# The first norm of an encoder trunk moves from the token rows to the results of the projections, and the first loads change order

## The chip, the core and the metric

The kernel runs on one core of a Trainium2 chip. The metric is device microseconds (us) of one execution; the time of a kernel is the median of its runs. Engines are named as the profile names them: PE multiplies matrices (PEld loads its stationary operand), ACT is the scalar engine, DVE the vector engine, POOL the third elementwise engine, and SP issues every DMA of this kernel. An engine works through its own instructions in order and waits on semaphores of others.

## What is computed

A two-layer encoder on 256 tokens of 1024 features. Only the start of layer 0 (the "even" layer) is touched:

```python
def rms_norm(x, g, eps=EPS):
    y = xf * lax.rsqrt(jnp.mean(xf * xf, axis=-1, keepdims=True) + eps)
    return (y * g.astype(jnp.float32)).astype(x.dtype)

def even_mixer(h, w_in, ...):
    proj = h @ w_in                                   # 1024 -> 1536 + 256 + 128 + 32
    hy, cq, ckv, kr = jnp.split(proj, [c0, c1, c2], axis=-1)
    hy = short_conv(hy, conv_w, conv_b)               # three taps along the tokens
    ...                                               # gated long convolution
    q = (rms_norm(cq, q_norm) @ w_uq)...              # latent attention, queries
    kv = (rms_norm(ckv, kv_norm) @ w_ukv)...          # keys and values
    k_pe = apply_rope(kr[:, :, None, :], cos_r, sin_r)
    ...

x = x + even_mixer(rms_norm(x, norm_mix[0]), ...)
x = x + cross_attention(rms_norm(x, norm_cross[i]), mem_n, ...)
x = x + sq_relu_mlp(rms_norm(x, norm_mlp[i]), ...)
```

After it come cross-attention to 256 memory tokens, an MLP of 4096, the same three blocks for layer 1 (differential attention in place of the even mixer), and a final norm. The norm is a factor per token, `rsqrt(mean(x²) + eps)`, times a gain per feature; a projection is linear, so the factor per token can be put on the projection's result.

## The kernel before

Every large product is made of three: each fp32 operand is split into a high part (rounded to a shorter mantissa, written by ACT, `split`, L104 to L106) and the rest (DVE, L106), and `mm3` (L108 to L112) issues high·high, high·low and low·high into one PSUM bank. A weight tile of up to 128×1024 is loaded by SP into one of four buffers `wraw` (`weight`, L87) and split into one of six pairs `whi`, `wlo`. SP therefore stands before a weight's load until the split of the fourth weight before it is done.

The 256 tokens lie as two tiles `xt[0]`, `xt[1]` of 128 rows (even and odd tokens) in buffers `t4`, of which there are three. For a projection the tokens have to stand transposed, features on the partitions: `h` is a pair (high, low) of 128 × 8 × 256, where index k is a block of 128 features and the last axis holds both token tiles.

PSUM has four banks `h` (function `hb`), three `b` (`wk`) and one `f`.

The stages of layer 0 are written in a string, `ORDER_EVEN` (L30), and issued in that order. A planner of the framework then places the instructions on the engines: it keeps that order as a priority, but an engine that by its own estimate of durations would stand idle gets a later instruction whose inputs are there. So the order on PE, ACT, DVE and SP is fixed when the kernel is built, and on the chip an engine waits for the instruction that is next, even if one behind it could run.

The stages at the start, in the order of the string:

- ahead of them: SP loads one row of gains (4 KB), both x tiles (512 KB each), `cpack` (identity and the gains by column, 92 KB), `c_rope`, the two latent gains `gq`. PE spreads the gain row over the partitions with a product with `ones` (L147) into two banks.
- `N` (`norm_in`): per token tile a Square with row sum on ACT (L183), two small POOL steps (`rstd_of`, L167 and L169), then DVE scales each half row by factor and gain in one step (L188); PE transposes four blocks of 128×128 (L175) and `split` evicts them, for features 0 to 511 of both token tiles.
- `G` (`filter_features`): loads `pack` (250 KB), two small products (L333, L337) each followed by a sine made of eight DVE steps and one ACT step.
- `J` (`lat_proj`): the latent projection, 416 columns, in four weight tiles of 416 KB (`w_lat`), each used for 12 matmuls; the features 512 to 1023 are transposed after the second weight (`mid`).
- `L` (`latents`): the two latent norms, the rotary of the shared key, transposes into `latT`.
- `H0` (`hy_chunk`): the first of six chunks of the Hyena projection, 256 columns each: two weight tiles, 48 matmuls into one bank, then per 128 channels one ACT step (L503) and four DVE steps (L506) of the short convolution, read from the bank.
- `U`, `K`, `R`: queries, keys and values, transposed queries. Later come scores and outputs of the eight heads (`S`, `O`), the filters (`F`, whose weight is `hy_w3`), the spectra (`P`), the other chunks (`H1` to `H5`), and `M`, which normalizes and transposes the memory with the same `normed` (L183, L188).

Of the kernel before, what the change touches and what calls it, by code (L numbers as in the profile page):

```python
# [17 lines left out]
P = 128  # L18
D = 1024
# [6 lines left out]
C2 = float(np.float32(TWO_PI - C1))  # L26
C3 = float(np.float32(TWO_PI - C1 - C2))
PI_LO = 3.1415925
# Order in which the stages are issued: a letter names the stage (see the run() calls), digits are its arguments.
ORDER_EVEN = "N G J L H0 U K R S0 D H1 F0 S1 T0 S2 S3 P0 O0 O1 O2 H2 S4 O3 H3 T1 F1 S5 S6 O4 O5 Y S7 H4 P1 H5 O6 O7 M W"  # L30
ORDER_CROSS = [
    "V0 K0 Q0 K1 S0 V1 B0 K2 S1 Q1 K3 W0 S2 B1 S3 V2 B2 V3 B3 W1",
    "K0 K1 Q0 V0 S0 S1 K2 B0 Q1 K3 S2 V1 B1 V2 B2 W0 V3 S3 B3 W1",
# [5 lines left out]
def tile_encoder(ctx: ExitStack, tc: tile.TileContext, a: dict, out: bass.AP):  # L39
# [17 lines left out]
    def hb():  # L57
        return T(ps, [P, 512], F32, "h", bufs=4)
# [10 lines left out]
    def t4(dt=F32):  # L69
        return T(ring, [P, 1024], dt, "t4", bufs=3)  # L70
# [10 lines left out]
    def col(n=1):  # L81
        return T(cst, [P, n], F32, f"col{n}", bufs=16)
# [1 line left out]
    def v3(t, k):  # L84
        return t.rearrange("p (k n) -> p k n", k=k)

    def weight(src, cols=1024, side=False, gi=None, nk=2):  # L87
        p_, x, nr, nw = (rp, "f", 2, 2) if side else (wp, "w", 4, 6)
        raw = T(p_, [P, 1024], F32, x + "raw", bufs=nr)[:, :cols]
        hi = T(p_, [P, 1024], F32R, x + "hi", bufs=nw)[:, :cols]  # L90
        lo = T(p_, [P, 1024], F32R, x + "lo", bufs=nw)[:, :cols]
        nc.sync.dma_start(raw, src)
        if gi is None:
            split(hi, lo, raw)
            return hi, lo
        gi, k0 = gi
        for k in range(nk):
            g = gcol[:, gi, k0 + k:k0 + k + 1]
            h_, l_, r_ = (v3(z, nk)[:, k, :] for z in (hi, lo, raw))
            nc.scalar.activation(h_, r_, AF.Identity, bias=zero, scale=g)  # L100
            nc.vector.scalar_tensor_tensor(l_, r_, g, h_.bitcast(F32), op0=ALU.mult, op1=ALU.subtract)  # L101
        return hi, lo
# [16 lines left out]
    es = ExitStack()  # L119
    ep = pool("ep", es)  # L120
    cur.update(pool=ep, n2=4)
# [2 lines left out]
    def load_x(dst):  # L124
        for t in range(2):
            nc.sync.dma_start(dst[t], xv[t])

    def const(p_, name, shape, src=None):
        t = T(p_, shape, F32, name)
        nc.sync.dma_start(t, a[name] if src is None else src)  # L130
        return t

    ones = T(ep, [1, P], F32, "ones")
    nc.gpsimd.memset(ones, 1.0)
    grow = t4()[0:1]
    nc.sync.dma_start(grow, a["gains"][0:1])
    xt = [t4(), t4()]
    load_x(xt)

    def gain(src):  # L140
        g = t4()
        nc.sync.dma_start(g, src.partition_broadcast(P))
        return g

    g_mix0 = [hb(), hb()]
    for c in range(2):
        nc.tensor.matmul(g_mix0[c], ones, grow[:, c * 512:(c + 1) * 512], start=True, stop=True)  # L147
    pack = const(cst, "cpack", [P, 184])
    ident = pack[:, :128]
    gcol = pack[:, 128:].rearrange("p (g k) -> p g k", k=8)  # L150
    packe = T(ep, [P, 500], F32, "pack")
# [9 lines left out]
    nc.gpsimd.memset(zero, 0.0)  # L161
    junk = T(cst, [P, D], BF16, "junk")

# [1 line left out]
    def rstd_of(ssq, n, dim, eps):  # L165
        r = col(n)
        nc.gpsimd.tensor_scalar(r, ssq, 1.0 / dim, eps, op0=ALU.mult, op1=ALU.add)  # L167
        r2 = col(n)
        nc.gpsimd.tensor_tensor(r2, r, mhalf[:, :n], op=ALU.pow)  # L169
        return r2  # L170
# [8 lines left out]
    def normed(xs, g):  # L179
        rs = []  # L180
        for x in xs:
            ssq = col()
            nc.scalar.activation(junk, x, AF.Square, accum_out=ssq)  # L183
            rs.append(rstd_of(ssq, 1, D, EPS))
        for t, x in enumerate(xs):
            for c in range(2):
                xc = x[:, c * 512:(c + 1) * 512]
                nc.vector.scalar_tensor_tensor(xc, xc, rs[t], g[c], op0=ALU.mult, op1=ALU.mult)  # L188

    def half_T(xs, h, c, bank=wk):  # L190
        for t, x in enumerate(xs):
            tr_split(x[:, c * 512:(c + 1) * 512], h, t, c, bank)
# [109 lines left out]
    def sin_of(b, bias, dst):  # L302
        y = h2(256)[:b.shape[0]]
        nc.vector.tensor_scalar(y, b, bias, fb[:b.shape[0], 2:3], op0=ALU.add, op1=ALU.mult)
# [96 lines left out]
    def softmax_e(sc, scale=None):  # L401
        s3 = v3(sc, 2)
        nm = col(2)
# [25 lines left out]
        else:  # L429
            split(dst, lo, b3)  # L430

    # ======== even mixer ========
    h = v3(t8(F32R), 8), v3(t8(F32R), 8)

    def tok_major(y):
# [13 lines left out]
    nc.sync.dma_start(gq[:, 256:], a["mla_kv_norm"].partition_broadcast(P))  # L449
    lat = []  # L450

    def norm_in():
        normed(xt, g_mix0)
        half_T(xt, h, 0)

    def lat_proj():
        lat.extend([wk(), wk()])
        proj_xs(h, a["w_lat"], 416, lat, mid=lambda: half_T(xt, h, 1), at=1)

    latT = [T(ep, [P, 3, 256], F32R, f"latT{i}") for i in range(2)]  # L460
    kT = v3(t8(), 8)
# [1 line left out]
    def latents():  # L463
        for t in range(2):
            ln = t2()
            ssq = col(2)
            nc.scalar.activation(ln[:, :256], lat[t][:, :256], AF.Square, accum_out=ssq[:, 0:1])
            nc.scalar.activation(ln[:, 256:384], lat[t][:, 256:384], AF.Square, accum_out=ssq[:, 1:2])
            rq = rstd_of(ssq[:, 0:1], 1, 256, EPS)
            rk = rstd_of(ssq[:, 1:2], 1, 128, EPS)  # L470
            nc.vector.scalar_tensor_tensor(ln[:, :256], lat[t][:, :256], rq, gq[:, :256], op0=ALU.mult, op1=ALU.mult)
            nc.vector.scalar_tensor_tensor(ln[:, 256:384], lat[t][:, 256:384], rk, gq[:, 256:], op0=ALU.mult, op1=ALU.mult)
            kp = T(ep, [P, 96], F32, "kp", bufs=2)
            nc.gpsimd.memset(kp[:, :64], 0.0)
            kr = lat[t][:, 384:416]
            tmp = T(ep, [P, 32], F32, "kptmp", bufs=2)
            nc.vector.tensor_tensor(tmp[:, :16], kr[:, 16:], SM[:, t, :16], op=ALU.mult)
            nc.vector.tensor_tensor(tmp[:, 16:], kr[:, :16], SM[:, t, 16:], op=ALU.mult)
            nc.vector.tensor_tensor(kp[:, 64:], kr, CM[:, t, :], op=ALU.mult)
            nc.vector.tensor_tensor(kp[:, 64:], kp[:, 64:], tmp, op=ALU.add)  # L480
            b = wk()
            for k in range(3):
                nc.tensor.transpose(b[:, k * P:(k + 1) * P], ln[:, k * P:(k + 1) * P], ident)
            nc.tensor.transpose(b[:96, 384:], kp, ident)
            sl = (slice(None), slice(0, 3), slice(t * P, (t + 1) * P))
            split(latT[0][sl], latT[1][sl], v3(b[:, :384], 3))
            nc.scalar.copy(kT[64:96, :, t * P:(t + 1) * P],
                           b[64:96, 384:].unsqueeze(1).to_broadcast([32, 8, P]))
# [3 lines left out]
    def hy_chunk(u):  # L492
        bank = hb if u < 4 else wk
        if u % 2 == 0:
            hyS[u // 2] = T(ep, [P, 4, 256], F32, "hy", bufs=2)
        b = bank()
        proj_w(h, a["w_hy"][u], b)
        for c in range(2):
            ct = 2 * u + c
            src = b[:, c * 256:(c + 1) * 256]  # L500
            y = hyS[ct // 4][:, ct % 4, :]
            w = [conv[:, j, ct:ct + 1] for j in range(4)]
            nc.scalar.activation(y, src, AF.Identity, bias=w[3], scale=w[1])  # L503
            e, o, ye, yo = src[:, :P], src[:, P:], y[:, :P], y[:, P:]
            for dst, s, wt in ((ye, o, w[2]), (yo, e, w[0]), (ye[:, 1:], o[:, :P - 1], w[0]), (yo[:, :P - 1], e[:, 1:], w[2])):
                nc.vector.scalar_tensor_tensor(dst, s, wt, dst, op0=ALU.mult, op1=ALU.add)  # L506
# [103 lines left out]
    def mla_proj():  # L610
        hs["b"] = [[wk(), wk()], [wk(), fl()]]
        proj_down(catm, (0, 1, 2, 3), a["w_out_ev"], (4, 5, 6, 7), hs["b"], True)

    run(ORDER_EVEN, S=mla_s, O=mla_o, H=hy_chunk, F=filters, T=toks, P=spec, Y=conv0, W=mla_proj, M=mem_T,
        N=norm_in, J=lat_proj, L=latents, G=filter_features, U=queries, K=keys_values, R=queries_T, D=tables)
    ys, banks = hs["y"], hs["b"]
    cat = [v3(t8(F32R), 8) for _ in range(2)]
    for u in range(2):
# [385 lines left out]
```

## Time and profile before

| | |
|---|---|
| median of 3 runs | 863.78 us (861.42, 863.78, 863.94) |
| profiled execution | span 861.4 us, beside the run of 861.42 us |
| PE busy | 841.5 us, 5326 matmuls |
| DVE busy | 567.4 us |
| ACT busy | 482.8 us |
| POOL busy | 21.4 us |
| DMA | 139.53 MB, mean 162 GB/s |

The span runs from the first to the last instruction. "Busy" sums the time in which an engine worked; PE's matmuls overlap in the records, so the distance from one start to the next says more of them than the duration of one. In a line of the timeline stand the start, the duration, the engine, the line of the kernel, the operation with output and inputs, how many instructions were merged, and in brackets how long the engine had been idle and what released it. In a line of groups, "x16 | 4.4, 275" means 16 instructions, 4.4 us in all, 275 ns each. A line of windows gives for each engine the busy us and the number of instructions in a stretch of time, then the granted PE clock (1.00 is full), the share of time in which the DMA engines worked, and the GB/s that they moved.

### The profile page before, as it was taken

Reading aid. Unit: us, or ns where it says so; the run is one execution under the profiler, and the core shown is the slowest. Engines: PE = TensorE matmul, PEld = TensorE weight load, DVE = VectorE, ACT = ScalarE, POOL = GpSimd, SP = SyncE. Lnnn points to the kernel's source line nnn. Section 1 sums busy time; section 2 is a strip of 40 time slices with the busy share of each in tenths; the row PEclk is TensorE's granted clock in tenths of the full one; section 3 lists DMA queues with packets and bytes.
Section 4 is the critical chain, followed back from the end, with each engine's and each line's share of the span. In section 5 each row is a group of like instructions: output and inputs, shape, how many; then the busy total and the mean of one; then the engine's idle time right before and its main releaser. Section 6 shows DMA issues by size and latency. Waiting matters only on the chain.

```text
span 861.4 us, 13548 instructions
## 1 busy us (share of the span) xinstructions
PE 841.5 (98%) x5326; PEld 742.0 (86%) x5326; DVE 567.4 (66%) x880; ACT 482.8 (56%) x784; POOL 21.4 (2%) x54
## 2 busy tenths in 40 slices
PE   6999999999999999999999999999999999999996
PEld 4967587999989999999988787789998999999995
DVE  5878986855557655655568889576564765565553
ACT  5864444755447555555467676675443755555542
POOL 0100000000000000000000010200000000000000
PEclk9999999999999999999999999999999999999998
DMA  7550317744344555555536524325432465555531
GB/s 259 201 216 18 118 43 276 259 157 154 117 147 173 195 189 183 191 191 182 191 126 222 171 99 155 139 99 196 149 121 74 167 201 181 187 195 183 185 121 49
DMA packets 39526, 139.53 MB, mean 162 GB/s; under 512 B 4515, under 2 KB 5283, under 8 KB 39462
## 3 DMA queue, kind: packets, MB, share of 16 engines
q1 hardware_dynamic: 39462, 138.66, 46.8%
q8 instruction: 42, 0.69, 0.3%
q14 instruction: 22, 0.18, 0.1%
HBM read 137.59 MB, written 1.05 MB: 161 GB/s over the span
## 4 chain that ended last, share of the span: by engine, by line
PE 86%; issue 7%; DMA 2%; ACT 2%; DVE 1%; POOL 1%; SPq 0%; POOLq 0%; ACTq 0%
PE h L110 14%; PE h L111 14%; PE h L112 14%; PE b L110 11%; PE b L111 10%; PE b L112 10%; PE f L110 2%; PE f L111 2%; PE f L112 2%; PE b L175 1%; DMA t<-in_hy_w_dram 1%; DMA pack<-in_pack_dram 1%; PE b L839 1%; PE b L426 1%; DMA wraw<-in_xa_wk_dram 1%
## 5 line engine op out<-in xcount | busy, mean ns | idle before, releaser
L106 DVE TENSOR_TENSOR wlo<-wraw,whi 128x1024 fp32r<-128x1024 f32 (+2 forms) x131 | 158.5, 1213 | 120.7 <-ACT whi L105 119.9
L105 ACT CAST whi<-wraw 128x1024 fp32r<-128x1024 f32 (+2 forms) x131 | 135.7, 1041 | 146.9 <-PE b L111 58.0
L100 ACT ACTIVATE whi<-wraw,zero,cpack 128x512 fp32r<-128x512 f32 x208 | 159.3, 809 | 66.9 <-PE b L111 33.3
L101 DVE SCALAR_TENSOR_TENSOR wlo<-wraw,cpack,whi 128x512 fp32r<-128x512 f32 x208 | 150.6, 750 | 54.5 <-ACT whi L100 54.2
L110 PE MATMUL b<-t,whi 128*128 128x256 f32 x544 | 154.3, 284 | 0.0
L112 PE MATMUL b<-t,wlo 128*128 128x256 f32 x544 | 154.1, 283 | 0.0
L111 PE MATMUL b<-t,whi 128*128 128x256 f32 x544 | 154.1, 283 | 0.0
L110 PEld LDWEIGHTS b<-t,whi 128*128 128x128 f32 x544 | 104.5, 192 | 0.9 <-issue 0.4
L111 PEld LDWEIGHTS b<-t,whi 128*128 128x128 f32 x544 | 104.5, 192 | 0.5
L112 PEld LDWEIGHTS b<-t,wlo 128*128 128x128 f32 x544 | 104.5, 192 | 0.0
L112 PE MATMUL h<-whi,ul 128*128 128x512 f32 x256 | 100.0, 390 | 0.0
L111 PE MATMUL h<-wlo,uh 128*128 128x512 f32 x256 | 99.9, 390 | 0.0
L110 PE MATMUL h<-whi,uh 128*128 128x512 f32 x256 | 99.9, 390 | 0.0
L110 PE MATMUL h<-whi,t 128*128 128x512 f32 x192 | 77.1, 402 | 0.0
L111 PE MATMUL h<-wlo,t 128*128 128x512 f32 x192 | 76.6, 399 | 0.0
L112 PE MATMUL h<-whi,t 128*128 128x512 f32 x192 | 76.0, 398 | 0.0
L112 PEld LDWEIGHTS h<-whi,ul 128*128 128x128 f32 x256 | 48.1, 188 | 9.9
L110 PE MATMUL h<-t,whi 128*128 128x256 f32 x192 | 55.8, 291 | 0.6 <-ACT t L105 0.6
L110 PEld LDWEIGHTS h<-whi,uh 128*128 128x128 f32 x256 | 48.2, 188 | 9.5
L111 PEld LDWEIGHTS h<-wlo,uh 128*128 128x128 f32 x256 | 48.1, 188 | 9.5
L111 PE MATMUL h<-t,whi 128*128 128x256 f32 x192 | 55.3, 288 | 1.0 <-DVE t L106 1.0
L112 PE MATMUL h<-t,wlo 128*128 128x256 f32 x192 | 55.4, 289 | 0.0
(287 smaller groups left out, 1549.2 us busy)
## 6 DMA issues: line engine op xcount, KB each, us to landing
wraw<-in_mlp_up_dram SPq DMA_DIRECT2D x64, 512.0 KB, 3.3
wraw<-in_mlp_down_dram SPq DMA_DIRECT2D x64, 512.0 KB, 3.2
wraw<-in_od_w_qkv_dram SPq DMA_DIRECT2D x24, 512.0 KB, 4.3
wraw<-in_xa_wq_dram SPq DMA_DIRECT2D x16, 512.0 KB, 4.3
wraw<-in_xa_wo_dram SPq DMA_DIRECT2D x16, 512.0 KB, 3.6
wraw<-in_w_hy_dram SPq DMA_DIRECT2D x12, 512.0 KB, 4.6
wraw<-in_w_out_ev_dram SPq DMA_DIRECT2D x8, 512.0 KB, 4.8
wraw<-in_xa_wv_dram SPq DMA_DIRECT2D x8, 512.0 KB, 4.9
```

Of the source, the lines that this page charges most:

```text
L100: nc.scalar.activation(h_, r_, AF.Identity, bias=zero, scale=g)
L101: nc.vector.scalar_tensor_tensor(l_, r_, g, h_.bitcast(F32), op0=ALU.mult, op1=ALU.subtract)
L105: nc.scalar.copy(hi, src)
L106: nc.vector.tensor_tensor(lo, src, hi.bitcast(F32), op=ALU.subtract)
L110: nc.tensor.matmul(o, lh, rh, start=first, stop=False)
L111: nc.tensor.matmul(o, lh, rl, start=False, stop=False)
L112: nc.tensor.matmul(o, ll, rh, start=False, stop=last)
L175: nc.tensor.transpose(b[:, k * P:(k + 1) * P], x[:, k * P:(k + 1) * P], ident)
L426: nc.tensor.transpose(b3[:, m, t * P:(t + 1) * P], p3[:, t, m * P:(m + 1) * P], ident)
L839: nc.tensor.matmul(ob[:, t * P:(t + 1) * P], aT[:, m, t * P:(t + 1) * P], vo[j][:, m, c * P:(c + 1) * P], start=m == 0, stop=m == 1)
```

## The change

The stage `N` goes; `J` now stands first in the order, ahead of `G`. The gains no longer come as a row: `cpack` is loaded first and its columns serve as the gain. The loads that follow are x tile 0, `w_lat` 0, x tile 1, `w_lat` 1, 2, 3; only then `c_rope`, `gq` and `pack`.

`tr_gain` transposes raw x, four blocks of 128×128 into one bank, and evicts each block by itself: ACT writes gain·x into the high part, DVE gain·x minus the high part into the low one. The factor of a token is not in `h` any more. After the last matmul of `J` it is computed (Square on ACT, `rstd_of` on POOL) as a column `rs0[t]` per token tile, and a product with the identity makes from it a tile `R` whose 128 rows all hold the 256 factors.

It then goes on the results. In `latents` (tokens on the partitions) the factor is the scale of the two Squares, is multiplied into the two latent factors on POOL, and enters the three rotary steps, which turn from a product of two into one of three. In `hy_chunk` (channels on the partitions) one DVE step per chunk multiplies the bank by `R` into an SBUF tile `un` of the pool `h2` (eight buffers), and the convolution reads `un` instead of the bank.

```diff
-ORDER_EVEN = "N G J L H0 U K R S0 D H1 F0 S1 ...
+ORDER_EVEN = "J G L H0 U K R S0 D H1 F0 S1 ...
...
-    ones = T(ep, [1, P], F32, "ones")
-    nc.gpsimd.memset(ones, 1.0)
-    grow = t4()[0:1]
-    nc.sync.dma_start(grow, a["gains"][0:1])
+    pack = const(cst, "cpack", [P, 184])
     xt = [t4(), t4()]
-    load_x(xt)
+    lat_raw = []
+    for i in range(4):
+        if i < 2:
+            nc.sync.dma_start(xt[i], xv[i])
+        lat_raw.append(fetch(a["w_lat"][i], 832))
...
-    g_mix0 = [hb(), hb()]
-    for c in range(2):
-        nc.tensor.matmul(g_mix0[c], ones, grow[:, c * 512:(c + 1) * 512], start=True, stop=True)
-    pack = const(cst, "cpack", [P, 184])
...
-    def norm_in():
-        normed(xt, g_mix0)
-        half_T(xt, h, 0)
+    R = T(ep, [P, 256], F32, "rrow")
+    rs0 = []
+
+    def tr_gain(t, c):
+        b = hb()
+        for k in range(4):
+            nc.tensor.transpose(b[:, k * P:(k + 1) * P], xt[t][:, (4 * c + k) * P:(4 * c + k + 1) * P], ident)
+        for k in range(4):
+            z, g = b[:, k * P:(k + 1) * P], gcol[:, 0, 4 * c + k:4 * c + k + 1]
+            hi, lo = (y[:, 4 * c + k, t * P:(t + 1) * P] for y in h)
+            nc.scalar.activation(hi, z, AF.Identity, bias=zero, scale=g)
+            nc.vector.scalar_tensor_tensor(lo, z, g, hi.bitcast(F32), op0=ALU.mult, op1=ALU.subtract)
 
     def lat_proj():
         lat.extend([wk(), wk()])
-        proj_xs(h, a["w_lat"], 416, lat, mid=lambda: half_T(xt, h, 1), at=1)
+        ws = []
+        for q in range(4):
+            tr_gain(q % 2, q // 2)
+            ws.append(weight(None, 832, raw=lat_raw[q]))
+            if q:
+                proj_x(h, ws[q - 1], 2 * (q - 1), 2, 416, lat, q == 1, False)
+        proj_x(h, ws[3], 6, 2, 416, lat, False, True)
+        for t in range(2):
+            ssq = col()
+            nc.scalar.activation(junk, xt[t], AF.Square, accum_out=ssq)
+            rs0.append(rstd_of(ssq, 1, D, EPS))
+        b = hb()
+        for t in range(2):
+            nc.tensor.matmul(b[:, t * P:(t + 1) * P], rs0[t].to_broadcast([P, P]), ident, start=True, stop=True)
+        nc.scalar.copy(R, b[:, :256])
...
-            nc.scalar.activation(ln[:, :256], lat[t][:, :256], AF.Square, accum_out=ssq[:, 0:1])
+            nc.scalar.activation(ln[:, :256], lat[t][:, :256], AF.Square, scale=r0, accum_out=ssq[:, 0:1])
...
+            for z in (rq, rk):
+                nc.gpsimd.tensor_tensor(z, z, r0, op=ALU.mult)
...
-            nc.vector.tensor_tensor(kp[:, 64:], kr, CM[:, t, :], op=ALU.mult)
+            for dst, z, tab in ((tmp[:, :16], kr[:, 16:], SM[:, t, :16]), (tmp[:, 16:], kr[:, :16], SM[:, t, 16:]),
+                                (kp[:, 64:], kr, CM[:, t, :])):
+                nc.vector.scalar_tensor_tensor(dst, z, r0, tab, op0=ALU.mult, op1=ALU.mult)
...
         proj_w(h, a["w_hy"][u], b)
+        un = h2()
+        nc.vector.tensor_tensor(v3(un, 2), v3(b, 2), R.unsqueeze(1).to_broadcast([P, 2, 256]), op=ALU.mult)
         for c in range(2):
             ct = 2 * u + c
-            src = b[:, c * 256:(c + 1) * 256]
+            src = un[:, c * 256:(c + 1) * 256]
```

`fetch` is the load of `weight` by itself; `weight` takes its result as `raw` and then only splits.

More of the change, by code (lines that the diff above doesn't have):

```diff
@@ L28 @@
 PI_LO = 3.1415925
-ORDER_EVEN = "N G J L H0 U K R S0 D H1 F0 S1 T0 S2 S3 P0 O0 O1 O2 H2 S4 O3 H3 T1 F1 S5 S6 O4 O5 Y S7 H4 P1 H5 O6 O7 M W"
+ORDER_EVEN = "J G L H0 U K R S0 D H1 F0 S1 T0 S2 S3 P0 O0 O1 O2 H2 S4 O3 H3 T1 F1 S5 S6 O4 O5 Y S7 H4 P1 H5 O6 O7 M W"
 ORDER_CROSS = [
@@ L85, in v3, with fetch, weight @@
         return t.rearrange("p (k n) -> p k n", k=k)
-    def weight(src, cols=1024, side=False, gi=None, nk=2):
+    def fetch(src, cols=1024):
+        raw = T(wp, [P, 1024], F32, "wraw", bufs=4)[:, :cols]
+        nc.sync.dma_start(raw, src)
+        return raw
+    def weight(src, cols=1024, side=False, gi=None, nk=2, raw=None):
         p_, x, nr, nw = (rp, "f", 2, 2) if side else (wp, "w", 4, 6)
-        raw = T(p_, [P, 1024], F32, x + "raw", bufs=nr)[:, :cols]
+        if raw is None:
+            raw = T(p_, [P, 1024], F32, x + "raw", bufs=nr)[:, :cols]
+            nc.sync.dma_start(raw, src)
         hi = T(p_, [P, 1024], F32R, x + "hi", bufs=nw)[:, :cols]
         lo = T(p_, [P, 1024], F32R, x + "lo", bufs=nw)[:, :cols]
-        nc.sync.dma_start(raw, src)
         if gi is None:
@@ L466, in latents @@
             ssq = col(2)
-            nc.scalar.activation(ln[:, :256], lat[t][:, :256], AF.Square, accum_out=ssq[:, 0:1])
-            nc.scalar.activation(ln[:, 256:384], lat[t][:, 256:384], AF.Square, accum_out=ssq[:, 1:2])
+            r0 = rs0[t]
+            nc.scalar.activation(ln[:, :256], lat[t][:, :256], AF.Square, scale=r0, accum_out=ssq[:, 0:1])
+            nc.scalar.activation(ln[:, 256:384], lat[t][:, 256:384], AF.Square, scale=r0, accum_out=ssq[:, 1:2])
             rq = rstd_of(ssq[:, 0:1], 1, 256, EPS)
             rk = rstd_of(ssq[:, 1:2], 1, 128, EPS)
+            for z in (rq, rk):
+                nc.gpsimd.tensor_tensor(z, z, r0, op=ALU.mult)
             nc.vector.scalar_tensor_tensor(ln[:, :256], lat[t][:, :256], rq, gq[:, :256], op0=ALU.mult, op1=ALU.mult)
@@ L476, in latents @@
             tmp = T(ep, [P, 32], F32, "kptmp", bufs=2)
-            nc.vector.tensor_tensor(tmp[:, :16], kr[:, 16:], SM[:, t, :16], op=ALU.mult)
-            nc.vector.tensor_tensor(tmp[:, 16:], kr[:, :16], SM[:, t, 16:], op=ALU.mult)
-            nc.vector.tensor_tensor(kp[:, 64:], kr, CM[:, t, :], op=ALU.mult)
+            for dst, z, tab in ((tmp[:, :16], kr[:, 16:], SM[:, t, :16]), (tmp[:, 16:], kr[:, :16], SM[:, t, 16:]),
+                                (kp[:, 64:], kr, CM[:, t, :])):
+                nc.vector.scalar_tensor_tensor(dst, z, r0, tab, op0=ALU.mult, op1=ALU.mult)
             nc.vector.tensor_tensor(kp[:, 64:], kp[:, 64:], tmp, op=ALU.add)
@@ L614, in tile_encoder @@
     run(ORDER_EVEN, S=mla_s, O=mla_o, H=hy_chunk, F=filters, T=toks, P=spec, Y=conv0, W=mla_proj, M=mem_T,
-        N=norm_in, J=lat_proj, L=latents, G=filter_features, U=queries, K=keys_values, R=queries_T, D=tables)
+        J=lat_proj, L=latents, G=filter_features, U=queries, K=keys_values, R=queries_T, D=tables)
     ys, banks = hs["y"], hs["b"]
```

## The prediction, made before the changed kernel ran

> **What bounds the kernel now.** I read the page first: the share of PE and its slices.
>
> ```profile
> span 861.4 us, 13548 instructions
> PE 841.5 (98%) x5326; PEld 742.0 (86%) x5326; DVE 567.4 (66%) x880; ACT 482.8 (56%) x784; POOL 21.4 (2%) x54
> PE   6999999999999999999999999999999999999996
> ```
>
> PE works in 98% of the span, and only the first slice (21.5 us) and the last are below nine tenths. So the change is worth what it takes from PE's gaps in the first slice, less what PE work it adds and what new gaps it makes later. Next I read PE's timeline there, then SP and ACT, and the chain of waits.
>
> ```profile
> 2.33 3.75 PE L147 MATMUL h<-t,ones 1*128 1x512 f32 x4 [2.33 <-DMA t<-in_gains_dram]
> 8.07 1.12 PE L175 MATMUL b<-cpack,t 128*128 128x128 f32 x4 [1.99 <-DVE t L188]
> 9.87 1.11 PE L333 MATMUL h<-pack 33*64 33x256 f32 x2 [0.68 <-DMA pack<-in_pack_dram]
> 10.91 1.11 PE L175 MATMUL b<-cpack,t 128*128 128x128 f32 x4
> 13.48 1.06 PE L110 MATMUL b<-whi,t 128*128 128x416 f32 x2 [1.46 <-ACT whi L105]
> 14.34 1.05 PE L175 MATMUL b<-cpack,t 128*128 128x128 f32 x4
> ...
> 16.24 0.55 PE L112 MATMUL b<-whi,t 128*128 128x416 f32 x1
> 16.58 0.55 PE L110 MATMUL b<-whi,t 128*128 128x416 f32 x1
> ...
> 17.41 0.35 PE L110 MATMUL b<-whi,t 128*128 128x416 f32 x1
> 17.59 0.35 PE L111 MATMUL b<-wlo,t 128*128 128x416 f32 x1
> ```
>
> ```profile
> 0.73 0.34 SPq L136 DMA_DIRECT2D t<-in_gains_dram  x1
> 1.13 0.83 SPq L126 DMA_DIRECT2D t<-in_x_dram  x2
> 2.00 0.43 SPq L130 DMA_DIRECT2D cpack<-in_cpack_dram  x1
> ...
> 4.39 3.11 SPq L92 DMA_DIRECT2D wraw<-in_w_lat_dram  x4
> ...
> 14.77 1.47 SPq L92 DMA_DIRECT2D wraw<-in_w_hy_dram  x2
> ```
>
> ```profile
> 5.16 1.06 ACT L183 ACTIVATE junk<-t 128x1024 bf16<-128x1024 f32 x1 [3.15 <-DMA t<-in_x_dram]
> ...
> 6.65 1.06 ACT L183 ACTIVATE junk<-t 128x1024 bf16<-128x1024 f32 x1 [0.34 <-DMA t<-in_x_dram]
> ...
> 15.92 1.67 ACT L105 CAST whi<-wraw 128x832 fp32r<-128x832 f32 x2
> ```
>
> The reader sees three things. First, PE's dense work begins at 13.48; ahead of it lie short pieces with gaps. Second, the x tiles are there at 5.16 and 6.65, so over 6 us go by on the norm (Square, POOL, L188), on `pack` (PE stands 0.68 us before L333, which the planner put between the two pairs of transposes) and on evictions. Third, two matmuls of 416 columns follow each other every 0.34 us at 16.24 but every 0.18 us from 17.41: PE runs its first dense stretch at half pace, from 13.48 to about 17.3.
>
> After this stage PE is full, so that what is won at the start is carried to the end unless a new gap opens:
>
> ```profile
> 8.00:12.00 4.00, 3.25 (x10) 1.71 (x10) 2.68 (x5) 0.58 (x1) 0.64 (x2) 1.00 0.98 387
> 16.00:20.00 4.00, 4.00 (x20) 3.92 (x19) 3.97 (x9) 3.38 (x5) 0.00 (x0) 1.00 0.84 273
> 25.00:30.00 5.00, 4.84 (x35) 4.30 (x34) 4.06 (x18) 3.49 (x10) 3.46 (x9) 1.00 0.31 110
> 30.00:40.00 10.00, 10.00 (x75) 9.81 (x75) 9.29 (x23) 9.28 (x17) 0.00 (x0) 1.00 0.68 227
> 50.00:55.00 5.00, 3.88 (x13) 1.95 (x12) 3.63 (x8) 2.42 (x3) 0.00 (x0) 1.00 1.00 381
> 70.00:75.00 5.00, 5.00 (x35) 3.94 (x34) 5.00 (x10) 1.42 (x2) 0.00 (x0) 1.00 0.19 56
> 75.00:80.00 5.00, 5.00 (x41) 4.84 (x40) 5.00 (x12) 1.51 (x2) 0.00 (x0) 1.00 0.00 0
> ```
>
> **The change part by part.**
>
> *Arrival.* SP issues `cpack` first and x tile 0 second, about where it stands now; 92 KB more lie ahead of it, 0.25 us at the 387 GB/s of the 8 to 12 window: 5.4 instead of 5.16. From tile 0 to tile 1 it took 1.49 us for 512 KB; `w_lat` 0 (416 KB) now lies between, 1.2 us more: `w_lat` 0 at 6.6, x tile 1 at 8.1 instead of 6.65. The other three weights follow 1.2 us apart, to 11.7; PE wants none of them so early.
>
> *First evictions.* Raw x goes to PE at once: four transposes 1.12, so tile 0 is in its bank at 6.5 and tile 1 at 9.2. The pieces of the eviction have no row of their own form; the nearest are these.
>
> ```profile
> L468 ACT ACTIVATE t<-b 128x128 f32<-128x128 f32 x2 | 0.5, 269 | 0.0
> L467 ACT ACTIVATE t<-b 128x256 f32<-128x256 f32 x2 | 0.8, 384 | 1.9 <-PE b L112 1.9
> L503 ACT ACTIVATE hy<-h,pack 128x256 f32<-128x256 f32 x8 | 4.5, 559 | 2.0 <-DVE hy L506 1.3 <-PE h L112 0.6
> L105 ACT CAST t<-b 128x512 fp32r<-128x512 f32 x36 | 20.8, 584 | 32.2 <-PE b L175 23.6 <-PE b L112 7.2 <-PE b L111 1.4
> L506 DVE SCALAR_TENSOR_TENSOR hy<-h,pack,hy 128x128 f32<-128x128 f32 x16 | 5.0, 346 | 2.1 <-ACT hy L503 2.0
> L106 DVE TENSOR_TENSOR wlo<-wraw,whi 128x832 fp32r<-128x832 f32 x4 | 4.0, 1008 | 0.0
> ```
>
> An ACT step with scale and bias from columns costs 0.175 more than a plain one of its shape (559 against 384 ns), so 128×128 costs 0.269 to 0.56, taken as 0.44; a DVE step 0.35 (L506, the same shape). Tile 0: ACT 6.5 to 8.3, `whi` 0 to 9.1; DVE's four low parts to 8.6, `wlo` 0 to 10.1. Tile 1: its first block is high at 9.65, low at 10.4 behind `wlo` 0. The first matmul can start at 9.1, and PE is continuously supplied from about 10.0. **Dense work starts at 10.0 instead of 13.48: 3.5 us won.** The bounds are 9.1 and 11.3: the latter if the planner puts the 1.25 us Square of tile 1 ahead of tile 1's evictions.
>
> *What PE has done by then.* Eight transposes, as before. The next four (14.34) can run from 9.2 to 10.0, in the gap; before, they took 0.85 of the dense stretch (next matmul after their start 0.71 to 1.05): **0.85 more**, bounds 0 and 1.05. L333 no longer runs in a gap: it follows in the dense stretch, at full pace half of 1.11: **0.55 back**. The L147 products vanish from a gap: nothing. `R` adds two products of 128×128 with a wait for `rs0`; the transposes L175 are of that shape, 0.28 each at half pace: **0.25 back**, bounds 0.1 and 0.6. Whatever PE has next stands behind that wait. The Squares (2.5 us) and POOL (about 0.8) after ACT's last `whi` at 17 give `rs0` at 20.4, ahead of the end of `J` near 21.5: no stall, and each us that ACT is later than that costs up to one.
>
> *ACT.* Sixteen steps of 0.44 take the place of four of 0.584: 4.7 us more, and 0.4 for the copy of `R`. With the four `whi` that is 10.4 us from 6.5, so the last `whi` of `J` is done at about 17, or 18.3 with a Square ahead of it; today it is done at 17.59. PE comes to the last 12 `w_lat` matmuls at about 19, so this is hidden; if ACT's order has both Squares (2.5 us) ahead, the cover is under 1 us. Behind it wait the splits of `w_hy`, whose loads are freed by `wlo` 0 and 1 and so leave SP near 10 and 12 instead of 14.77. In 16 to 30 ACT had 3.3 us idle by the windows (16 to 20 and 25 to 30 quoted, 20 to 25 had 1.2), enough for most of the rest. I put 0.2 for a stall here, bounds 0 and 2.
>
> *Latents.* POOL gets four small products, DVE's three rotary steps a factor more.
>
> ```profile
> L167 POOL TENSOR_SCALAR col<-col 128x1 f32<-128x1 f32 x8 | 2.0, 250 | 89.5 <-ACT junk L183 72.8 <-ACT t L467 16.5
> L169 POOL TENSOR_TENSOR col<-col,mhalf 128x1 f32<-128x1 f32 x8 | 4.6, 574 | 0.7
> ```
>
> Two in a row per tile at 0.25 to 0.57 lengthen the chain to `latT` by 0.5 to 1.1 per tile, and the DVE step for the latent waits behind them, with the transposes of `latT` on PE behind that. H0 covers it: 48 matmuls, and PE was full in 30 to 40. Nothing, with a price of up to 2.2 if H0's weights are late. The Squares wait for `rs0`, four PE groups earlier: nothing.
>
> *The chunks.* Six `un` steps, DVE from a bank, 128×512:
>
> ```profile
> L358 DVE TENSOR_TENSOR h<-h,t 128x512 f32<-128x512 f32 x4 | 2.7, 684 | 1.4 <-PE h L356 1.4
> L309 DVE SCALAR_TENSOR_TENSOR h<-h,h 128x256 f32<-128x256 f32 x3 | 1.3, 420 | 0.0
> L471 DVE SCALAR_TENSOR_TENSOR t<-b,col,gq 128x256 f32<-128x256 f32 x2 | 1.0, 484 | 0.5 <-POOL col L169 0.5
> ```
>
> That is 4.1 us. A step of the same shape from SBUF instead of a bank is 64 ns shorter (420 against 484); if that holds for the 48 convolution steps, 3.1 come back. The first step also waits for `R`, and on DVE the next `wlo` parts stand behind it (H0's bank is done long after `R`, so nothing). DVE was full in 70 to 80, where chunks H2 and H3 lie, so there the net may show: 0.25, bounds 0 and 1.4.
>
> *Queues.* `c_rope`, `gq`, `pack` go behind 1.70 MB of `w_lat`: 4.4 us later at 387 GB/s. `pack` was there at 9.8, now at about 14.2; its first reader L333 comes later in PE's order, the latents read the others past 20. SP does not wait until the fifth weight.
>
> **Sum:** −3.5 − 0.85 + 0.55 + 0.25 + 0.2 + 0.25 = **−3.1 us**. The profiled execution would go from 861.4 to 858.3. It is the fastest of three; the median is 863.78, so the forecast is **860.7**.
>
> **A rule against the trace.** The windows give a granted clock of 1.00 before and after 17.3, so the doubling of pace is not in that number; it is only in the distance of the matmuls. The Trainium skill, "TensorE: Matmul & The Clock Gate", Part 1 (the HAM clock gate), says that the array starts at half clock and is released after a busy window of about 3.4 us that runs freely, not from the first matmul. The 3.8 us in the trace agree. By that rule the half-paced stretch could last up to 6.8 us.
>
> **The rivals.**
>
> *A, the forecast*, with its own range 859.2 to 862.2.
>
> *B, more is won.* Nothing stalls later, or PE reaches full pace soon after 10: each us of half pace less saves 0.5. With the 9.1 start and no later terms the sum is −4.4 (−4.4 − 0.85 + 0.55 + 0.25); with 1 us less at half pace −4.9: 858.9. Against an early full pace: between 8 and 12 PE was busy 3.25 us and stayed slow.
>
> *C, the slow stretch does not move with the start.* If pace is released at 17.3 again, PE runs 3.5 us longer at half pace and loses 1.7 of the gain: −1.4, 862.4. For it: only one change of pace is in the trace, so its cause can't be told. The rule above allows it.
>
> *D, ACT becomes the bound* from 17 to 30, by the Squares and the sixteen steps: the 2 us bound in place of 0.2 gives −1.3, 862.5.
>
> *E, it is given back at the filter weight.* PE waits there, and DMA is full in 50 to 55:
>
> ```profile
> 44.36 7.16 DMA t<-in_hy_w_dram
> ```
>
> If that landing is set by the bytes ahead of it, not by its issue, PE waits 3.1 longer there: 863.8. Against it: the load ahead of it on SP waits for a buffer that PE frees, so the issue moves with PE.
>
> *F, slower: PE stands before `pack`.* If the planner puts L333 into the gap between the transposes of tile 0 and tile 1, as it does today, PE waits until 14.2, is through at 15.3, then has tile 1's transposes (1.1) and first eviction (0.8): dense at 17.2, so +3.7 − 0.85 + 0.25 + 0.45 = +3.6 (L333 is in a gap again): 867.3. If L333 lies behind the first `w_lat` matmuls, it does nothing. Against it: J now stands ahead of G, and the planner put L333 behind tile 0's transposes though PE was idle from 6.1 to 8.1, so it does reckon with a late `pack`.
>
> **How the numbers follow.** About 0.3% (2.6 us) can be told from no change, so the lines are at 861.2 and 866.4. A 0.52, of which two thirds lie below 861.2 (0.35) and 0.17 above; B 0.13, faster; C 0.10, D 0.10, E 0.05, no change; F 0.10, slower. Faster 0.48, same 0.42, slower 0.10. The range leaves out F and the far ends of A and B: 857.5 to 864.5.
>
> **What would show it.** The first `w_lat` matmul near 9.1 and one every 0.34 us from 10; the 0.18 us pace near 14 (C: near 17); the last `w_lat` matmul near 21.5; L333 behind the first `w_lat` matmuls (F: ahead of them, with a wait for `pack`); PE full from 20 to 40 (D: waits for ACT); the first PE wait for `hy_w3` no longer than 1.1 (E: 4). It is wrong if PE's new order leaves gaps after 20 that no row here shows.

## The result: the changed kernel is slower by one part in a hundred

| | before | changed |
|---|---|---|
| median | 863.25 us (861.42 to 863.94, 4 runs) | 871.85 us (871.43 to 872.30, 4 runs) |
| ratio, with 95% interval | 1 | 1.0104 [1.0087, 1.0121] |
| span of the profiled execution | 861.4 us | 869.6 us |

The ratio is 9.0 us of 862.5, about the time of the kernel before (from here on, a ratio is turned into us in this way). The forecast was 860.7, and the range ended at 864.5.

The page of the changed kernel, with busy times and the slices of PE and of its granted clock:

```profile
span 869.6 us, 13589 instructions
...
PE 842.4 (97%) x5326; PEld 744.4 (86%) x5326; DVE 571.4 (66%) x894; ACT 488.0 (56%) x797; POOL 22.4 (3%) x57
...
PE   6799999999999999999999999999999999999996
...
PEclk9799998999999999999999999999999999999998
```

PE has the same 5326 matmuls and about the same busy time (841.5 before). So 7.3 of the 8.2 us of span are time in which PE stood (27.2 us against 19.9). The place is in the slices: the second (21.7 to 43.5 us) is down to 7 of 10, with the granted clock at 7 as well, and the clock has a second dent in the seventh (130 to 152 us). Before, PE's second slice had a 9.

The start itself went as hoped. PE's timeline, changed kernel:

```profile
6.18 1.08 PE L461 MATMUL h<-cpack,t 128*128 128x128 f32 x4 [6.18 <-DMA t<-in_x_dram]
8.53 1.54 PE L461 MATMUL h<-cpack,t 128*128 128x128 f32 x6 [1.26 <-DMA t<-in_x_dram]
9.72 0.69 PE L116 MATMUL b<-whi,t 128*128 128x416 f32 x1
...
11.63 0.44 PE L117 MATMUL b<-wlo,t 128*128 128x416 f32 x1
11.90 0.35 PE L118 MATMUL b<-whi,t 128*128 128x416 f32 x1
...
20.23 0.61 PE L483 MATMUL h<-cpack,col 128*128 128x128 f32 x4
20.76 0.64 PE L336 MATMUL h<-pack 33*64 33x256 f32 x2
21.34 0.45 PE L118 MATMUL b<-whi,t 128*128 128x416 f32 x1
22.85 0.45 PE L512 MATMUL b<-cpack,t 128*128 128x128 f32 x2 [1.06 <-DVE t L500]
...
25.63 0.45 PE L513 MATMUL b<-cpack,kp 128*96 128x128 f32 x1 [1.41 <-DVE kp L509]
...
29.32 1.22 PE L340 MATMUL h<-h,pack 64*128 64x256 f32 x2 [2.18 <-ACT h L314]
30.47 0.58 PE L116 MATMUL h<-t,whi 128*128 128x256 f32 x1
30.85 0.41 PE L117 MATMUL h<-t,whi 128*128 128x256 f32 x1
...
35.33 0.35 PE L116 MATMUL h<-t,whi 128*128 128x256 f32 x1
35.51 0.28 PE L117 MATMUL h<-t,whi 128*128 128x256 f32 x1
```

`J` begins at 9.72, runs at 0.19 us per matmul from about 11.6 on, and starts its last matmul at 21.34. Before, the last one started at 26.11:

```profile
26.11 0.35 PE L112 MATMUL b<-whi,t 128*128 128x416 f32 x1
```

There the changed kernel is 4.8 us ahead, though the second product of `G`, which the kernel before has done by then (L337 at 21.92), is still to come. Then PE does next to nothing for 9 us: its next instructions are the transposes of the latents (L512, L513) and the second product of `G` (L340), and each waits for a chain on DVE, ACT and POOL. Only at 30.47 come the products of `H0`, though the low part of their second weight was written by 21.3. This is the **first hole**. The windows say the same (PE, PEld, DVE, ACT, POOL, then the granted clock), changed kernel, then the kernel before:

```profile
12.00:16.00 4.00, 4.00 (x23) 3.96 (x22) 3.85 (x10) 4.00 (x10) 0.00 (x0) 1.00 0.97 330
16.00:20.00 4.00, 4.00 (x23) 3.95 (x22) 2.78 (x7) 3.97 (x7) 0.75 (x2) 1.00 0.81 288
20.00:30.00 10.00, 4.75 (x19) 2.48 (x17) 7.43 (x22) 8.44 (x17) 4.57 (x12) 0.76 0.33 112
30.00:40.00 10.00, 10.00 (x59) 9.53 (x58) 7.77 (x15) 4.02 (x6) 0.00 (x0) 0.73 0.55 181
```

```profile
20.00:30.00 10.00, 9.84 (x62) 8.62 (x61) 7.47 (x22) 7.29 (x18) 3.55 (x9) 1.00 0.54 178
```

PE is busy for 4.75 of the 10 us from 20 to 30 (9.84 before), and up to 35.3 it pays once more: the 20 products of `H0` from 30.85 to 35.33 take 4.48 us, which at the 0.12 us from 35.51 on would be 2.4. The first query product starts at 38.63, before at 33.27. So 4.8 us ahead has become 5.4 behind.

A **second hole** lies a hundred us later. PE's waits there, changed kernel:

```profile
130.12 0.71 PE L655 MATMUL h<-c_dft,h 128*128 128x128 f32 x4 [2.03 <-DVE h L397]
131.93 0.79 PE L656 MATMUL h<-c_dft,h 128*128 128x128 f32 x2 [1.09 <-DVE h L398]
```

These are the products that turn the second spectrum back (before: L626, L627, no wait). They wait for its DVE steps. DVE's timeline, changed kernel; the two halves of the spectrum start at L347, and L397 is one of its last steps:

```profile
114.25 1.23 DVE L112 TENSOR_TENSOR wlo<-wraw,whi 128x1024 fp32r<-128x1024 f32 x1 [1.88 <-ACT whi L111]
116.17 0.69 DVE L528 TENSOR_TENSOR h<-b,rrow 128x512 f32<-128x512 f32 x1 [0.70 <-PE b L118]
...
120.37 1.28 DVE L347 TENSOR_TENSOR h<-h,h 128x512 f32<-128x512 f32 x2
...
129.39 0.68 DVE L397 TENSOR_TENSOR h<-h,h 128x512 f32<-128x512 f32 x1
```

and of the kernel before (L344 is the same step as L347, L394 as L397):

```profile
101.11 0.69 DVE L344 TENSOR_TENSOR h<-h,h 128x512 f32<-128x512 f32 x1
...
117.87 0.68 DVE L394 TENSOR_TENSOR h<-h,h 128x512 f32<-128x512 f32 x1
```

The last of the products that the halves read, on PE of the changed kernel:

```profile
105.70 1.02 PE L381 MATMUL h<-z,c_dft 128*128 128x512 f32 x2
```

So the halves could have run from about 107 on; they start at 120.37, before at 101.11. In between DVE stands idle (1.88 and 0.70 us in these lines), so it is not short of time. The halves stand behind `un` of chunk `H4` (116.17) and its convolution, and from there on DVE is the bound: 10.00 of the 10 us from 120 to 130.

### The profile page after: what moved, and what is told of

It reads as the page before. It is cut to its first block, busy times and chain, and to the rows that moved or that the text cites. A ratio compares the mean times of both kernels' runs of the same rounds, so it can differ in the third digit from the quotient of the medians.

```text
span 869.6 us, 13589 instructions
## 1 busy us (share of the span) xinstructions
PE 842.4 (97%) x5326; PEld 744.4 (86%) x5326; DVE 571.4 (66%) x894; ACT 488.0 (56%) x797; POOL 22.4 (3%) x57
## 4 chain that ended last, share of the span: by engine, by line
PE 89%; DVE 3%; DMA 3%; ACT 2%; POOL 1%; issue 1%; SPq 0%; POOLq 0%; ACTq 0%
PE h L116 14%; PE h L117 14%; PE h L118 14%; PE b L116 11%; PE b L117 11%; PE b L118 11%; PE f L116 2%; PE f L118 2%; PE f L117 2%; PE b L178 1%; DMA fraw<-in_xa_wk_dram 1%; DMA t<-in_x_dram 1%; PE b L593 1%; PE b L601 1%; DMA t<-in_hy_w_dram 1%
```

## The experiments

**Theory P (claims).** An instruction that takes a fresh bank or buffer stands, in its engine's order, behind the claims that come ahead of it in the string, since one name's buffers are handed out in that order. `G` and `H0` both take banks `h`. With `J` ahead of `G`, the second product of `G`, which waits for a sine, comes at `J`'s end and holds `H0` behind it: first hole. `un` takes a buffer of `h2`, of which there are eight and the second spectrum takes that many; `H4` stands ahead of that spectrum (`P1`) in the string, so the spectrum waits for `H4`: second hole. **Rival W (work).** The sixteen steps of 128×128 and the `un` steps make ACT and DVE late, and PE's waits are the result. A third reading of the first hole, that `H0` waits for a bank `h` that is still in use, does not fit the trace: by 22 us all banks taken ahead of it had been read, but for that of the late product itself (the last gain step ends at 20.2, the copy of `R` at 21.2, the first read of `G`'s first product at 22.0).

### One claim moved at a time

First `e1`, the products of `G` in the single bank `f`:

```diff
 (in filter_features, both products of G)
-        b = hb()
+        b = fl()
```

> The changed kernel with one edit: the two banks of G come from the single bank f instead of the four banks h. Theory P (claims stand in the order of the string): H0's bank no longer waits behind G's second product, H0's matmuls stand behind the last w_lat matmul on PE, the hole from 21.8 to 30.5 goes; the first query matmul moves from 38.6 to about 30; 864.5 us (863 to 866.5), the second hole near 120 to 131 stays. Theory W (more work: sixteen ACT steps, longer latent chain on POOL): the hole stays within 1 us of its size, 870.5 to 872.5.

866.38 us, ratio 1.0048 [1.0030, 1.0066]: of 9.0 us over the kernel before, 4.1 are left. Window and PE's wait, this run:

```profile
20.00:30.00 10.00, 9.46 (x70) 8.72 (x68) 7.86 (x23) 7.45 (x16) 4.15 (x12) 1.00 0.40 122
```

```profile
30.84 0.70 PE L340 MATMUL f<-h,pack 64*128 64x256 f32 x2 [1.37 <-ACT h L314]
```

The same work stands on ACT and DVE, yet PE is busy for 9.46 instead of 4.75. The second product of `G` is even later than in the changed kernel (30.84 against 29.32), but nothing of `H0` waits behind it. That is P for the first hole. The second was left as it was (waits of 2.0 and 1.1 us).

Then `e2`, `un` without a buffer of its own:

```diff
-        un = h2()
-        nc.vector.tensor_tensor(v3(un, 2), v3(b, 2), R...)
+        nc.vector.tensor_tensor(v3(b, 2), v3(b, 2), R...)
...
-            src = un[:, c * 256:(c + 1) * 256]
+            src = b[:, c * 256:(c + 1) * 256]
```

> The changed kernel with one edit: the step that multiplies by R writes back into the PSUM bank instead of into a buffer h2, and the convolution reads the bank; DVE has the same number of steps. Theory P: the second spectrum no longer stands behind H4's buffer, its halves start near 106 on DVE instead of 120, PE's waits of 2.0 and 1.1 us for it go: 868 us (867 to 869.5), the first hole stays. Theory W: the six steps themselves fill DVE, the waits stay: 871 to 872.5.

869.23 us, 1.0083 [1.0064, 1.0101]: 1.8 us less than the changed kernel, though the two intervals overlap, so this pair alone does not tell the gain from nothing. The waits for L397 and L398 are gone (one of 0.59 for L398 is left) with the same number of DVE steps. But the spectrum did not come forward as P said. Only its first half starts early, at 108.36; the second starts at 120.16, behind `H4` as in the changed kernel, and L397 at 129.13 (129.39 in the changed kernel). What moved is PE's work: the forward products of the second half (L380, L381) stand at 116.83 instead of 104.84, so PE reaches the end of the chain later and waits less for it. `e3` has both edits:

> The changed kernel with both edits (G's banks from f, the product with R written back into the bank). Theory P: both holes go, what was won at the start is kept: 860.5 us (859 to 862.5), faster than the kernel before. Theory W: 870.5 to 872.5.

865.08 us, 1.0025 [1.0010, 1.0041]: 6.8 us less than the changed kernel, about the sum of both (4.8 + 1.8). But the gain over the kernel before that was expected did not appear.

### The same two holes made in the kernel before

`e4` puts only `J` ahead of `G`; norm, gain and loads stay. `e11` does the same with `G`'s products in bank `f`.

```diff
-ORDER_EVEN = "N G J L H0 U ...
+ORDER_EVEN = "N J G L H0 U ...
```

> The kernel before with one edit: in the string G stands behind J (N J G L instead of N G J L); no work is added or removed and the loads keep their order. Theory P: H0's bank is now claimed behind a late second product of G, H0's matmuls stand behind it on PE and a hole opens between the end of the latent projection and H0: 867.5 us (865.5 to 871). Theory W: no work changed, 862 to 864.5.

> The kernel before with two edits: G stands behind J (as in the run that swapped them), and G's banks come from f, so that H0's bank is not claimed behind them. Theory P: the first product of G leaves the gap between the two pairs of transposes, J begins at about 11.5 instead of 13.5, and no hole opens: 861.2 us (860 to 862.5), 7 to 10 below the run that only swapped. If the swap itself costs (latents late): 864 or more.

`e4` took 870.45 us, 1.0083 [1.0064, 1.0103]; `e11` 861.7 us, 1.0003 [0.9990, 1.0016]. PE's timeline of `e4`, then of `e11`:

```profile
25.86 0.35 PE L112 MATMUL b<-whi,t 128*128 128x416 f32 x1
27.64 0.44 PE L483 MATMUL b<-cpack,t 128*128 128x128 f32 x2 [1.42 <-DVE t L471]
...
30.69 0.70 PE L337 MATMUL h<-h,pack 64*128 64x256 f32 x2 [0.58 <-ACT h L311]
...
31.45 0.56 PE L110 MATMUL h<-t,whi 128*128 128x256 f32 x1
```

```profile
26.21 0.35 PE L112 MATMUL b<-whi,t 128*128 128x416 f32 x1
26.39 0.28 PE L112 MATMUL h<-t,wlo 128*128 128x256 f32 x1
...
31.04 0.70 PE L337 MATMUL f<-h,pack 64*128 64x256 f32 x2 [0.58 <-ACT h L311]
```

In `e4` `J` ends at 25.86, the same waits follow, and `H0` comes only behind L337. In `e11` `H0` follows `J` at once, with L337 even 0.35 us later than in `e4` and none of the changed kernel's steps in it. Between the two lie 6.9 us by the ratios: the claim alone is worth that, the half-paced products behind the hole included. It also shows that `J` ahead of `G` gains nothing by itself in the kernel before.

`e7` and `e8` add only a step of the size of `un` to the kernel before: a copy of the bank into a buffer `h2` from which the convolution reads, or of the bank onto itself.

```diff
+        un = h2()                             (e7)
+        nc.vector.tensor_copy(un, b)          (e7)
+        nc.vector.tensor_copy(b, b)           (e8)
```

> The kernel before with one edit: each of the six chunks is copied by DVE from its bank into a buffer h2 and the convolution reads that copy (no factor, the result is the same). Theory P: the second spectrum stands behind H4's buffer as in the changed kernel, PE waits for its chain at about 118 to 127: 865.5 us (864 to 867.5). Theory W: six DVE steps of 0.69, of which most hide: 862 to 863.5.

> The kernel before with the same six DVE steps, but each copies the bank onto itself, so no buffer h2 is claimed. Theory P: the price of the steps alone, 862.2 to 863.5, at least 2 us below the run with the copy into h2. Theory W: the same time as that run within 1 us.

`e7`: 866.15 us, 1.0031 [1.0018, 1.0044]; `e8`: 863.93 us, 1.0007 [0.9997, 1.0018]. PE's waits of `e7`:

```profile
125.99 0.71 PE L626 MATMUL h<-c_dft,h 128*128 128x128 f32 x4 [2.03 <-DVE h L394]
127.79 0.80 PE L627 MATMUL h<-c_dft,h 128*128 128x128 f32 x2 [1.09 <-DVE h L395]
```

They are the changed kernel's two waits, to the hundredth of a us, in a kernel that has nothing else of the change. So the copy into a buffer costs 2.1 us more than the copy onto the bank; the work of the six steps costs 0.6, which their interval does not tell from nothing. How the buffer does it is only in part what P said. DVE's timeline of `e8`, which takes no buffer (the second half's L344, then L394):

```profile
115.02 0.68 DVE L344 TENSOR_TENSOR h<-h,h 128x512 f32<-128x512 f32 x1
...
124.00 0.68 DVE L394 TENSOR_TENSOR h<-h,h 128x512 f32<-128x512 f32 x1
```

In `e7` these start at 116.23 and 125.25, in the kernel before at 104.23 and 117.87. So the chain is late in `e8` too, by all but 1.25 us; why its second half stands behind `H4` without a buffer was not settled. The difference that the traces show is on PE. In `e8` the second half's forward products run at 111.69, ahead of the chain's end, not at 100.70; PE waits 0.8 and 0.6 us at two places far apart, and its clock is 1.00 in each window of 2 us from 126 to 132. In `e7` the waits of 2.03 and 1.09 follow each other, and the clock of those three windows is 0.94, 0.50 and 0.71.

### What was left once the holes were closed

`e5` closes the first hole in another way (`G` ahead of `J` in the string, its products in `f`, `un` in its bank). `e6` adds that both x tiles are loaded ahead of the four weights, and `e9` is the changed kernel with that alone.

```diff
-ORDER_EVEN = "J G L H0 U ...        (e5, e6)
+ORDER_EVEN = "G J L H0 U ...        (e5, e6)
...
+    load_x(xt)                      (e6, e9)
     for i in range(4):
-        if i < 2:                   (e6, e9)
-            nc.sync.dma_start(xt[i], xv[i])
```

> The changed kernel with three edits: G stands ahead of J in the string as it did before, its banks come from f, and the product with R is written back into the bank. G's sine chain then starts during J instead of behind it, so its second product is no longer late for PE (in the run with both edits PE still waited 1.4 us for it at 29.2). Theory P: PE is full from the latent projection on, the 3 us won at the start are kept: 860 us (858.5 to 862.5). Theory W (the longer latent chain and ACT's sixteen steps bound the stage in any order): no better than the run with both edits, 864 to 866.

> The kernel of the run before with one edit: both x tiles are loaded ahead of the four w_lat tiles instead of in turn with them. x tile 0 alone at the head of the queue should land near 5.3 as in the kernel before (6.0 to 6.8 in turn), x tile 1 near 6.8 (8.2 to 9.0 in turn), w_lat 0 near 8. If the loads in turn cost the start: dense work begins up to 1 us earlier, 0.5 to 1.5 us faster than the run before. If they help or do nothing, within 0.7 us or slower.

> The changed kernel with one edit: both x tiles ahead of the four w_lat tiles. With the two holes left in, the start is all that moves: in the pair of runs before, this order let PE begin its dense stretch at 9.9 instead of 12.2 and gave 2.7 us. If the loads in turn are a cost of their own: 868.5 to 870.5 against 871.85 for the changed kernel. If the hole swallows whatever the start brings: 871 to 872.5.

`e5`: 866.13 us, 1.0031 [1.0017, 1.0044], no better than `e3`. `e6`: 863.46 us, 1.0001 [0.9989, 1.0013]. `e9`: 868.38 us, 1.0076 [1.0062, 1.0089]. The loads in turn, part of the change, cost 2.6 us (`e5` to `e6`) and 2.4 us (changed kernel to `e9`).

The traces show two parts of the 2.6. Tile 0 came no earlier in `e6` (first transpose at 6.20, in turn 6.18 to 6.79, where 5.3 was expected), but tile 1 did: `e6` runs its sixteen transposes without a wait, and supply becomes continuous at 10.90 instead of 12.16. And `e5` lost its clock once: PE waits 1.08 us for L340 at 25.36, and soon after its products run at half pace, a loss of 1.7 us by the windows of 1 us. In `e6`, with a wait of 0.75 there, the clock stays at 1.00. One window of `e5`:

```profile
28.00:30.00 2.00, 2.00 (x12) 2.00 (x11) 1.64 (x7) 1.57 (x2) 1.63 (x5) 0.50 0.01 4
```

`e6` equals the kernel before, and it still shows PE waiting in the query products, 29.6 to 36.5. `e10` takes the gain out of it: the evictions become plain ones of 128×512, as in the kernel before, and the gain of the first norm is left out of the computation.

```diff
-        for k in range(4):
-            z, g = b[:, k * P:(k + 1) * P], gcol[:, 0, 4 * c + k:4 * c + k + 1]
...
+        split(h[0][sl], h[1][sl], v3(b, 4))
```

> The kernel with x tiles first, G ahead of J with its banks from f and the product with R in the bank, with one edit: each eviction is one plain split of 128x512 on ACT and DVE, four of each instead of sixteen; the gain of the first norm is left out of the computation. Theory W for what is left (the sixteen steps put ACT and DVE behind, so PE waits for the query weights and for evictions between 30 and 40): 860 to 862.3, at least 1.2 us below 863.46. If claims alone set the time: 862.8 to 864.

860.68 us, 0.9984 [0.9971, 0.9997]: the first one below the kernel before, by 1.4 us. It lies 1.5 below `e6`, whose interval overlaps with this one, so that difference is at the edge of what can be told. PE's waits in `e6`:

```profile
31.30 0.44 PE L117 MATMUL b<-wlo,latT 128*128 128x384 f32 x1 [0.55 <-DVE wlo L112]
33.46 0.44 PE L116 MATMUL b<-whi,latT 128*128 128x384 f32 x1 [0.86 <-ACT t L515]
51.69 2.81 PE L358 MATMUL h<-t,aT 128*128 128x512 f32 x6 [1.46 <-DMA t<-in_hy_w_dram]
```

and of `e10`, which has no wait in the query products:

```profile
48.58 2.81 PE L358 MATMUL h<-t,aT 128*128 128x512 f32 x6 [0.35 <-DMA t<-in_hy_w_dram]
```

In `e6` ACT is still at the last gain step at 20.45; in `e10` it has stood idle for 2.28 us when it begins the norms of the latents at 20.19. So W, which fell for the first hole, may hold for a rest of about 1.5 us: the steps of the gain make ACT and DVE late, and PE waits in the query products ten us later. `e10` takes the steps out of both engines at once, so it does not say which of them counts.

Last, `e12` keeps the gain but applies it to a whole bank at once, on DVE, ahead of plain evictions:

```diff
+        xg = v3(t2(), 4)
+        nc.vector.tensor_tensor(xg, v3(b, 4), gcol[...].to_broadcast([P, 4, P]), op=ALU.mult)
+        split(h[0][sl], h[1][sl], xg)
```

> The changed kernel with both x tiles loaded ahead of the weights, G's products ahead of J in banks f, the kernel's result written back into its own bank, and the gain of the first norm applied to a whole bank of four transposes by one VectorE product of 128x512 into a buffer of its own, ahead of two plain evictions of 128x512, one on each engine, in place of the sixteen steps of 128x128. It computes all that the changed kernel computes. Theory W (what was left over was the many small steps of the eviction): the four products cost VectorE about four times 0.6 us in the first 10 us but ScalarE's eight small steps become four longer ones, so the U products run at nearly the pace of the run without the gain: 861.3 us, at least 1 us below the 863.46 of the run with sixteen steps, and a little below the kernel before. Rival (the extra pass puts VectorE late for the second half of the transposes and the latents): 863 us or more.

862.67 us, 1.0001 [0.9990, 1.0011]: the rival's 863 is nearer than 861.3. It is no gain over `e6` (1.0001 too) and none over the kernel before. Of the waits in the query products only one, of 0.48 us, is left, so those waits alone do not explain what `e10` gained. No version that computes everything beat the kernel before.

## Why the prediction was wrong, step by step

*Arrival*: mis-sized. Tile 0 was forecast 0.24 us later than before; ACT had it at 6.07 instead of 5.16, 0.9 later, and about as late when no weight was loaded behind it (6.09 in `e6`). With tile 1, forecast at 8.1, PE began at 8.53. The order of the loads was taken as given: the sum holds no term for it, and it costs 2.4 to 2.6 us.

*First evictions* and *What PE has done by then*: the Square of tile 0 stands ahead of tile 0's first eviction on ACT (6.07 to 7.2), which the text had reckoned with only for tile 1. A mean step took 481 and 346 ns for the forecast 440 and 350 (groups by line and shape, changed kernel):

```profile
L465 ACT ACTIVATE t<-h,zero,cpack 128x128 fp32r<-128x128 f32 x16 | 6.6, 481 | 0.9 <-PE h L461 0.7
```

```profile
L466 DVE SCALAR_TENSOR_TENSOR t<-h,cpack,t 128x128 fp32r<-128x128 f32 x16 | 4.9, 346 | 8.8 <-ACT t L465 8.8
```

Supply became continuous at 11.4 to 11.6, later than 10.0 and than the bound of 11.3, but PE was at its full pace from about 11.6, not from 14. The two errors cancel, and that is luck: `J` starts its last matmul at 21.34, and 21.5 was forecast. In `e1`, with the same instructions up to there, the full pace came at 14.3 and the last matmul started at 22.86 (0.5 of that is tile 1, which came later). `R` (20.23) took 0.53 us for the 0.25 taken, inside its bounds, the first product of `G` (20.76) 0.58 for 0.55; neither waited.

*ACT*: the cover by `J` held. ACT was full from 12 to 20 (4.00 and 3.97 of 4), and PE did not stand there. What the steps cost came behind `J`, where the text had 0.2 (bound 2): 1.5 us by `e10`, with the doubt said there.

*Latents*: **this step failed.** "H0 covers it … Nothing" took the work of `H0` as a cover without asking whether PE could reach it. It could not: L340 stood ahead. The code had it: the prediction moved L333 and priced it (0.55), and left out that `G`'s second product, L337, moves as well and takes a bank of the same name as `H0`. Price 4.8 us (`e1`), 6.9 in the kernel before (`e4`, `e11`).

*The chunks*: **this step failed too.** `un` was priced as work (0.25), while its buffer was taken as free. The work is about that (0.6, not told from nothing); with a buffer of its own it costs 2.1 us more (`e7` against `e8`), by PE's waits and the lost clock shown there. The 3.1 us that shorter convolution steps might bring back did not come: they take 345 ns from `un` and 346 from the bank.

*Queues* and rivals: F (a stand before `pack`) did not come: L336 ran at 20.76 without a wait. Slower came by another way than the rival for slower. C did not come either: in no trace of a version of the changed kernel did the full pace come later than 14.4. B's early full pace was there in the profiled execution, but not in `e1`. E stayed far below the 3.1 us that it gave back: PE waits for `hy_w3` 1.1 us before, 0.34 in the changed kernel, where PE came late, 1.46 in `e6` and 2.1 in `e3`.

Added up by ratios: 9.0, less 6.8 for the claims (`e3`), gives 2.2; `e5` stands at 2.7; less 2.6 for the loads gives 0.1; less 1.5 without the gain and its steps gives −1.4 [−2.5, −0.3]. The forecast was −3.1. The sum that the prediction made is thus there in its sign and about half its size, in a kernel that leaves the gain out. Why the rest is missing was not settled; candidates in `e10`'s trace are PE's waits for DVE between 80 and 125, which were not tested by themselves.

## What to carry to other kernels

When a stage is moved, list every bank and buffer that it takes, by name, and who takes the next one of that name: a waiting instruction holds those behind it even if their inputs are there. A new buffer of a name that is in use is a place in a queue, not only memory; look for a way to write back in place or to use another name. A chain that ends late costs little as long as PE has other work placed ahead of it (`e8`): look at what PE has to do, and not only at when the chain ends. "Hidden behind work X" is a claim about order: check that X can run at that moment.

## What the runs showed of the hardware that was not expected

**Short waits in a row halve PE's clock, with a delay.** Windows of 2 us, changed kernel; the column behind the five engines is the granted clock:

```profile
22.00:24.00 2.00, 0.56 (x3) 0.32 (x3) 1.19 (x5) 2.00 (x6) 1.51 (x7) 1.00 0.93 291
24.00:26.00 2.00, 0.59 (x2) 0.18 (x2) 2.00 (x10) 1.20 (x2) 1.68 (x5) 0.80 0.29 119
26.00:28.00 2.00, 1.14 (x4) 0.47 (x3) 1.89 (x7) 1.86 (x3) 0.23 (x1) 0.50 0.01 4
...
34.00:36.00 2.00, 2.00 (x14) 2.00 (x13) 2.00 (x4) 1.13 (x2) 0.00 (x0) 0.64 0.38 152
```

If the clock is either 1.00 or 0.50, 0.80 puts the drop at 25.2 and 0.64 the return at 35.4, which is where the distance of the products goes from 0.21 to 0.12. The drop comes 3.4 us after `J`'s last product was done at 21.8, the return 4.9 us after `H0` began. The Trainium skill, "TensorE: Matmul & The Clock Gate", Part 1, names two states, half and full, with changes after an idle or a busy window of about 3.4 us that runs freely. The trace agrees with the two states and with delays of that size. It differs in that PE need not stand idle for a whole window: no wait in the hole is longer than 2.18 us, short products lie between, and in `e5` one wait of 1.08 us, with PE busy for 0.92 of the 2 us from 24 to 26, was followed by half pace from about 26.8 to 30.2.

**When the full pace comes at the start differs from execution to execution.** In the profiled run of the changed kernel it came at about 11.6, 3.1 us after PE's work had become continuous at 8.53. In `e1`, with the same instructions up to there, it came 5.2 us after (9.04 to about 14.3):

```profile
13.74 0.55 PE L116 MATMUL b<-whi,t 128*128 128x416 f32 x1
...
14.36 0.35 PE L118 MATMUL b<-whi,t 128*128 128x416 f32 x1
```

In `e9` it came 6.3 us after (6.43 to 12.7), in the kernel before 3.8 us into the dense stretch. Transposes are enough: in `e10`, which begins them at 6.71, the last of the sixteen take 273 ns, the median 421, and no dense product had run yet.

**A run's time follows its mean clock.** Of `e10`'s runs those with a mean clock of 0.997 or 0.998 took 859.6 us in the mean (7 runs), those with 0.994 or 0.995 862.5 (5). A single profile is thus no measure of a gain of 2 us; the ratios above rest on 4 to 12 runs of each changed version.
